# A hybrid attention block on one core: the first MLP in two blocks of two tiles, beside single tiles of projection and memory attention

## The chip, the core and the metric

The kernel runs on one NeuronCore of a Trainium2 chip. Five engines work side by side, each on a queue of its own: TensorE (PE; its weight loads are listed apart as PEld), VectorE (DVE), ScalarE (ACT), GpSimd (POOL) and SyncE (SP), which here only issues DMAs. The metric is the device time of one execution in microseconds. Before the change three runs gave 1806.28 to 1810.84 us, with a median of 1808.53.

## What is computed

One transformer block on x of 1024 tokens by 1024 features, in float32:

```
for l in range(DEPTH):
    x = x + _hybrid_mixer(_rms_norm(x, norm1_g[l]), w_in[l], ..., w_out[l])
    x = x + _memory_xattn(_rms_norm(x, norm2_g[l]), mem, mem_norm_g[l], w_xq[l], w_xk[l], w_xv[l], ..., w_xo[l])
    x = x + _sq_relu_mlp(_rms_norm(x, norm3_g[l]), w_ff_in[l], w_ff_out[l])
```

The mixer has eight heads of indexed sparse attention (for each query the 256 keys with the best index score) and eight heads of block sparse attention in three branches (compressed, selected, window). Its output goes through `w_out` (1024 by 1024). Memory attention has four heads of 128 over 256 memory rows. The MLP is

```
def _sq_relu_mlp(h, w_ff_in, w_ff_out):
    return jnp.square(jax.nn.relu(h @ w_ff_in)) @ w_ff_out
```

with matrices of 1024 by 4096 and 4096 by 1024.

## The kernel before

**Tiles and precision.** Tokens go in eight tiles of 128 rows. A product that needs more than one pass of `fp32r` splits both operands into a high part and a rest: three matmuls, high by high, high by rest, rest by high. `split_w` makes the two parts of a weight: a copy on one engine, and a subtraction on another. The pairs come in turn from a plan; in `PLAN_MAIN` it is ScalarE for the copy ("a") and GpSimd for the subtraction ("g"). `load_w` does this after a DMA of 256 KB into `wraw`. Products for which a weight is not split (`load_whole`) use plain float32 matmuls on the loaded weights; those of `between` and `memory` are such.

**Stages.** `project` of tiles 0 to 3 runs alone. Then `attend` makes attention tile by tile, with the index scores and the top-256 search of the next tile beside it (`index_mask`). The generator `fill` supplies work to stand beside attention: `project` of tiles 4 to 7, `memory` (keys and values of the memory rows, kept in DRAM as `KX` and `VX`), `between` for tiles 0 and 1, `between` for 2 and 3, `mlp` for tiles 0 to 3, `between` for 4 and 5. What `fill` has left when attention ends runs in the tail, together with `between` for tiles 6 and 7, and then `mlp` for tiles 4 to 7.

**`between`** (line 894) takes a stretch of tiles from the attention output in DRAM (`oT_dr`) to the input of the MLP: the product with `w_out` and the residual (`add_to`, line 891), the norm and its transposes (`norm_T2`), the query product with `w_xq`, memory attention for pairs of heads (`memory_item`), a round trip of its output through DRAM (`xo_dr`), and the product with `w_xo`.

**`mlp`** (line 994) runs eight groups of 512 hidden features. For each it computes the hidden features of all its tiles, 24 matmuls of 128x512 for 128 features (three parts by eight slices of 128 input features), then ReLU and square on ScalarE (lines 1026, 1027) and the split on GpSimd (1029, 1030). Then come the two halves of the output, 12 matmuls of 128x512 for each tile, added to the residual.

**Order.** Every stage is a generator that yields an amount of work after each step. `together` steps through attention and lets `fill` go on while its amount is at most attention's times the pace. A tuple from `fill`, `(need, pace)`, holds it until attention is past tile `need`, and sets the new pace. `beside` and `merge` step through two generators in proportion to given totals; in the tail `REST` = 70 stands against 45. The instructions are recorded in that order and then arranged by the framework's scheduler; on the chip each engine runs its own queue in order.

**Memory.** `RINGS` gives the number of buffers for each name in a pool. `dn` holds `fill`'s stages from `memory` on, `d2` the tail's. Accumulators in PSUM are rings too: `dn` uses `psD` (two) and `psM` (one), attention `psS`, `psPT` and `psPV`; in the tail `d2` uses `psS` and `psPT`.

Of the kernel before, what the change touches and what calls it, by code (L numbers as in the profile page):

```python
# [10 lines left out]
F32R = mybir.dt.float32r  # L11
# [32 lines left out]
PLAN_HEAD = ("ag", "av")  # L44
PLAN_MAIN = ("ag",)
PLAN_TAIL = ("ag", "av", "ag")
# [32 lines left out]
TC_ARGS = {"schedule_with_timeline_sim": True}  # L79
PACES = (1.35, 1.35, 1.35, 1.75, 1.75)  # L80
REST = 70.0

# [26 lines left out]

def together(att, fill, projected):  # L110

# [4 lines left out]
    while la:  # L116
        held = part > len(projected)
        if lead is None and need < tile_:
            lead = df - da * pace
        if lf and need < tile_ and (held or df <= lead + da * pace):  # L120
            w = next(fill, None)
            lf = w is not None
            if isinstance(w, tuple):
                need, pace = w
                lead = None
            else:
                df += w or 0.0
        else:
            assert not held
            x = next(att, None)  # L130
            la = x is not None
            if la and x[1] is None:
                part += 1
            elif la:
                tile_ = x[0]
                da += x[1]
# [30 lines left out]
def build(nc, tc, I, C, out):  # L167
# [159 lines left out]

    def xT(pool, nt, whole=False):

        parts = [pool.tile([P, DM // P, nt * P], F32 if whole else F32R, tag="x" + n, name="x" + n)  # L330
                 for n in ("h" if whole else "hl")]
        return (parts, [lambda t, k, x=x: x[:, k, t * P:(t + 1) * P] for x in parts],
# [661 lines left out]
    def mlp(pool, t0, nt, x2s):  # L994
# [13 lines left out]
        for f4 in range(8):  # L1008
# [24 lines left out]
            for c in range(2):  # L1033
# [4 lines left out]
                for t in range(nt):  # L1038
# [12 lines left out]
                    yield 2.6  # L1051

    def pe_stack():
        pe = p1.tile([P, 2, 32], F32, tag="pe", name="pe")
# [33 lines left out]
    aw = aw_pool.__enter__()  # L1088
    projected = []

    def fill():
# [17 lines left out]
    together(attend(aw, st), rest, projected)  # L1109
    aw_pool.__exit__(None, None, None)  # L1110
# [32 lines left out]
```

## Time and profile before

| | |
|---|---|
| median of 3 runs | 1808.53 us |
| profiled execution | 1807.76 us, its span 1806.0 us |
| granted TensorE clock, mean | 0.976 |
| attention's first value product of tiles 0 to 7 | 162, 215, 304, 415, 542, 718, 929, 1155 us |
| last value product of attention | 1304 us |
| DMA traffic | 185.38 MB, mean 103 GB/s |

Times in the profile are microseconds of one execution, unless marked ns; L with a number is a line of the kernel before. Engine rows give busy time, its share of the span and the count of instructions. The slices divide the span into 40; a digit is the busy share in tenths. Rows of windows give, for each stretch, its length, the busy time of each engine with the count of instructions in brackets, then the clock that the throttle granted to TensorE as a share of full speed, the busy share of the DMA engines, and GB/s. Rows of groups name the line, engine and operation, output<-inputs, shapes and count, then the busy time, the mean of one in ns, and the idle time just before them with what ended it. Timeline rows give start, duration, instruction and count; in square brackets is the idle time before it. DMA rows give the KB of each and the median time from issue to landing. Matmuls are pipelined: their distance is read from the starts, not from the mean duration.

### The profile page before, as it was taken

The numbers are of one execution on the slowest core, as the hardware profiler recorded it, in microseconds if no ns is written. First come the engines' busy times: TensorE is split into PE (matmuls) and PEld (weight loads), VectorE is DVE, ScalarE is ACT, GpSimd is POOL, SyncE is SP. The second block draws the span as 40 slices with busy tenths as digits, with TensorE's granted clock in tenths as the row PEclk, the third lists the DMA queues.
The fourth block names the chain that finished last, engine by engine and source line by source line (L and its number), as shares of the span: only waits on it lengthen the run. The fifth ranks groups of instructions, "written<-read, shape, count | busy, mean of one in ns | idle before, by whom it ended". The sixth has DMA issues, their size and how long they took to land. (4 is left out here: it accounts for less than half of the span.)

```text
span 1806.0 us, 27690 instructions
## 1 busy us (share of the span) xinstructions
PE 1700.2 (94%) x9134; PEld 1447.8 (80%) x9134; DVE 927.8 (51%) x2343; ACT 1061.9 (59%) x2655; POOL 887.4 (49%) x1015
## 2 busy tenths in 40 slices
PE   5987999899989999999998999999999799999998
PEld 5986888688878777788886888888888687787887
DVE  4545757665874776375754555646524322222221
ACT  4445669797688579855896558994513333333332
POOL 2356647363541355568575667662111144545444
PEclk9998999999999999999999999999999799999999
DMA  6235221366336211212122212226384122222222
GB/s 193 73 121 155 70 68 58 114 196 175 102 109 196 87 59 42 75 65 80 59 75 75 62 65 78 65 74 194 98 284 151 47 87 89 97 91 96 94 95 93
DMA packets 171887, 185.38 MB, mean 103 GB/s; under 512 B 26464, under 2 KB 140896, under 8 KB 171744
## 3 DMA queue, kind: packets, MB, share of 16 engines
q1 hardware_dynamic: 163808, 173.13, 30.3%
q0 software_dynamic: 7936, 10.49, 2.2%
q8 instruction: 72, 1.18, 0.3%
q14 instruction: 71, 0.58, 0.1%
HBM read 162.59 MB, written 20.97 MB: 102 GB/s over the span
## 5 line engine op out<-in xcount | busy, mean ns | idle before, releaser
L249 POOL TENSOR_TENSOR wlo<-wraw,whi 128x512 fp32r<-128x512 f32 (+1 forms) x231 | 310.6, 1351 | 280.9 <-ACT whi L244 252.9
L244 ACT ACTIVATE whi<-wraw 128x512 fp32r<-128x512 f32 (+2 forms) x289 | 181.0, 628 | 250.8 <-PE psS L218 156.8
L218 PE MATMUL psD<-whi,xh 128*128 128x256 f32 (+1 forms) x704 | 191.1, 352 | 4.4 <-ACT whi L244 3.4
L218 PE MATMUL psD<-wlo,xh 128*128 128x256 f32 (+1 forms) x704 | 190.3, 352 | 1.6 <-DMA wlo<-in_w_in_dram 1.0
L236 DVE TENSOR_TENSOR pl<-psPT,ph 128x512 fp32r<-128x512 f32 (+1 forms) x232 | 142.1, 621 | 78.9 <-ACT ph L235 76.3
L218 PE MATMUL psD<-whi,h 128*128 128x512 f32 x512 | 174.3, 403 | 3.7 <-ACT whi L244 1.6
L218 PE MATMUL psS<-whi,h 128*128 128x512 f32 x512 | 162.4, 392 | 5.4 <-DVE b L891 5.4
L680 ACT ACTIVATE S<-S,mn 128x128 f32<-128x128 f32 (+7 forms) x192 | 142.7, 744 | 40.5 <-DVE mn L678 39.0
L685 POOL TENSOR_SCALAR S<-S,sums,gi 128x640 f32<-128x640 f32 (+7 forms) x128 | 107.8, 853 | 114.1 <-DVE sums L683 103.5
L235 ACT ACTIVATE ph<-psPT 128x512 fp32r<-128x512 f32 (+1 forms) x232 | 122.9, 540 | 61.5 <-PE psPT L695 57.1
L249 DVE TENSOR_TENSOR wlo<-wraw,whi 128x512 fp32r<-128x512 f32 (+1 forms) x58 | 56.3, 971 | 170.3 <-ACT whi L244 170.1
L218 PEld LDWEIGHTS psD<-wlo,xh 128*128 128x128 f32 x704 | 132.4, 193 | 13.6 <-DMA wlo<-in_w_in_dram 1.4
L218 PEld LDWEIGHTS psD<-whi,xh 128*128 128x128 f32 x704 | 130.0, 193 | 14.2 <-ACT whi L244 3.8
L695 PE MATMUL psPT<-c_ident,S 128*128 128x128 f32 x816 | 131.8, 277 | 3.9 <-POOL S L685 2.6
L891 DVE TENSOR_TENSOR b<-psS,b 128x512 f32<-128x512 f32 (+1 forms) x80 | 49.9, 636 | 138.5 <-PE psS L218 138.5
L218 PE MATMUL psS<-K,qh 128*128 128x384 f32 (+3 forms) x288 | 112.4, 394 | 8.9 <-DVE mn L678 3.9
L218 PEld LDWEIGHTS psS<-whi,h 128*128 128x128 f32 x512 | 96.0, 188 | 30.4 <-DVE b L891 10.1
L218 PEld LDWEIGHTS psD<-whi,h 128*128 128x128 f32 x512 | 95.5, 189 | 25.8 <-ACT whi L244 2.0
L695 PEld LDWEIGHTS psPT<-c_ident,S 128*128 128x128 f32 x816 | 97.6, 142 | 14.1 <-POOL S L685 4.5
L218 PE MATMUL psD<-wlo,h 128*128 128x512 f32 x256 | 102.6, 404 | 1.1 <-POOL wlo L249 1.1
L218 PE MATMUL psD<-xh,wlo 128*128 128x512 f32 x256 | 101.5, 398 | 0.0
L891 DVE TENSOR_TENSOR b<-psD,b 128x512 f32<-128x512 f32 (+1 forms) x112 | 63.2, 573 | 74.0 <-PE psD L218 66.9
(289 smaller groups left out, 4546.2 us busy)
## 6 DMA issues: line engine op xcount, KB each, us to landing
wraw<-in_w_ff_in_dram SPq DMA_DIRECT2D x128, 256.0 KB, 2.7
wraw<-in_w_ff_out_dram SPq DMA_DIRECT2D x128, 256.0 KB, 2.6
whi<-in_w_out_dram SPq DMA_DIRECT2D x32, 256.0 KB, 3.8
wlo<-in_w_out_dram SPq DMA_DIRECT2D x32, 256.0 KB, 4.3
wraw<-in_w_in_dram SPq DMA_DIRECT2D x24, 256.0 KB, 3.4
q<-st SPq DMA_DIRECT2D x12, 512.0 KB, 2.6
qin<-q SPq DMA_DIRECT2D x44, 128.0 KB, 2.3
x<-in_x_dram SPq DMA_DIRECT2D x8, 512.0 KB, 5.5
```

Source lines behind the costliest of these rows:

```text
L218: te.matmul(o, a, b, start=start, stop=stop)
L235: s.activation(hi, src, AF.Copy)
L236: v.tensor_tensor(lo, src, hi, op=ALU.subtract)
L244: s.activation(hi, raw, AF.Copy)
L249: (v if l == "v" else g).tensor_tensor(lo, raw, hi, op=ALU.subtract)
L680: s.activation(S, S, AF.Exp, bias=low, scale=-1.0, accum_out=sums[:, hh:hh + 1])
L685: g.tensor_scalar(Ss[hh], Ss[hh], sums[:, hh:hh + 1], 1.0 if gate is None else gate[:, hh:hh + 1], op0=ALU.mult, op1=ALU.mult)
L695: te.transpose(p2[:, j, hh, :], S[:, (c + j) * P:(c + j + 1) * P], ident)
L891: v.tensor_tensor(dst, pt, dst, op=ALU.add)
```

## The change

The first MLP, for tiles 0 to 3 in one pass, becomes two passes of a new function `mlp2`, each for two tiles. `fill` calls `between` for tiles 0 and 1, keeps their residuals in SBUF, and then runs `two_streams`: the main stream is `mlp2` for tiles 0 and 1 and then for 2 and 3; the side stream is `between` for one tile at a time, 2, 3, 4 and 5. The second `mlp2` starts when tiles 2 and 3 are through, and tiles 4 and 5 wait for that start. A side tile starts when attention is past it (`seen["tile"]`). Steps of the two streams are recorded in proportion to their amounts (`SIDE` = 0.9). What is not done when attention ends goes to the tail, against `between` for tiles 6 and 7 and the first 4.0 units of the last MLP.

Beside that: the paces of the last stages go from 1.75 to 1.5, `REST` from 70 to 110; whole weights in `dn` get a ring of their own of two buffers (`wb`) in place of `whi` and `wlo` with four each; `mlp2` has its own rings for the hidden features (`hs`, `mr`); in `PLAN_MAIN` every third subtraction goes to VectorE; and `between` loads attention's output straight into the tile that later holds the norm's transposes.

```diff
-    "dn": {"b4": 4, "h": 8, "relu": 2, "wraw": 2, "whi": 4, "wlo": 4},
+    "dn": {"b4": 4, "h": 7, "hs": 8, "mr": 2, "relu": 2, "wb": 2, "wraw": 2, "whi": 4, "wlo": 4},
-PLAN_MAIN = ("ag",)
+PLAN_MAIN = ("ag", "av", "ag")
-PACES = (1.35, 1.35, 1.35, 1.75, 1.75)
-REST = 70.0
+PACES = (1.35, 1.35, 1.35, 1.5, 1.5)
+SIDE = 0.9
+REST = 110.0
...
-        raw = ring(pool, ("whi", "wlo")[wholes["i"] % 2], shape)
+        raw = ring(pool, "wb" if "wb" in RINGS.get(pool.name, ()) else ("whi", "wlo")[wholes["i"] % 2], shape)
...
     def between(pool, t0, nt, x2s, keep):
-        o_of = []
+        one = "b" if nt == 1 else "h"
+        (o,), xf, _ = xT(pool, nt, True, one)
         for t in range(nt):
-            o = ring(pool, "b4", [P, 8, P])
             for c in range(8):
-                nc.sync.dma_start(o[:, c, :], oT_dr[t0 + t][c])
-            o_of.append(o)
+                nc.sync.dma_start(o[:, c, t * P:(t + 1) * P], oT_dr[t0 + t][c])
...
-        yield from gemm(pool, [lambda t, k: o_of[t][:, k, :]], 8, nt, W["w_out"], four, add_to)
-        _, xf, xt_of = xT(pool, nt, True)
+        yield from gemm(pool, xf, 8, nt, W["w_out"], four, add_to)
+        _, xf, xt_of = xT(pool, nt, True, one)
...
+    def mlp2(pool, t0, x2s):
+        x2 = [x2s[t0], x2s[t0 + 1]]
+        (xh, xl), _, xt_of = xT(pool, 2)
+        gb3 = gain2(pool, W["norm3_g"])
+        for t in range(2):
+            norm_T2(pool, x2[t], gb3, xt_of(t))
+            yield 1.0
+        for f4 in range(8):
+            hs = []
+            for f2 in range(2):
+                gr = []
+                c0 = (f4 * 4 + f2 * 2) * P
+                for k0 in range(0, 8, KG):
+                    hi, lo = load_w(pool, [P, KG, 256], (lambda r: r, W["w_ff_in"][k0 * P:(k0 + KG) * P, c0:c0 + 256]
+                                                         .rearrange("(k p) n -> p k n", p=P)))
+                    gr += [(hi[:, k, :], lo[:, k, :]) for k in range(KG)]
+                for f in range(2):
+                    pt = pst(TAGS[pool.name][0], [P, 256])
+                    fs = slice(f * P, (f + 1) * P)
+                    for k in range(8):
+                        wh, wl = gr[k]
+                        mm(pt, wh[:, fs], xh[:, k, :], k == 0, False)
+                        mm(pt, wl[:, fs], xh[:, k, :], False, False)
+                        mm(pt, wh[:, fs], xl[:, k, :], False, k == 7)
+                    hh, hl = ring(pool, "hs", [P, 256], F32R), ring(pool, "hs", [P, 256], F32R)
+                    r = ring(pool, "mr", [P, 256])
+                    s.activation(r, pt, AF.Relu)
+                    s.activation(r, r, AF.Square)
+                    g.tensor_scalar(hh, r, 1.0, 1.0, op0=ALU.mult, op1=ALU.mult)
+                    g.tensor_tensor(hl, r, hh, op=ALU.subtract)
+                    hs.append((hh, hl))
+                    yield 2.6
+            for c in range(2):
...
+                    gr.append(load_w(pool, [P, 512], (lambda r: r, W["w_ff_out"][r0:r0 + P, cs])))
+                for t in range(2):
+                    pt = pst(TAGS[pool.name][0], [P, 512])
...
+                    v.tensor_tensor(x2[t][:, cs], pt, x2[t][:, cs], op=ALU.add)
...
+                    yield 2.6
...
-        yield from between(dn, 0, 2, {}, False)
-        yield 3, PACES[2]
         x2s = {}
-        yield from between(dn, 2, 2, x2s, True)
-        yield 3, PACES[3]
-        yield from mlp(dn, 0, 4, x2s)
-        yield 5, PACES[4]
-        yield from between(dn, 4, 2, {}, False)
+        yield from between(dn, 0, 2, x2s, True)
+        yield seen["tile"] - 1, PACES[2]
+        yield from two_streams(dn, x2s)
+
+    def two_streams(dn, x2s):
+        main, mains = mlp2(dn, 0, x2s), 1
+        side, t = None, 2
+        dm = ds = 0.0
+        while main or side or mains < 2 or t < 6:
+            if side is None and t < 6 and seen["tile"] > t and (t < 4 or mains == 2):
+                side, ds = between(dn, t, 1, x2s, t < 4), dm
+                if t == 4:
+                    yield seen["tile"] - 1, PACES[3]
+            if main is None and mains == 1 and side is None and t >= 4:
+                main, mains = mlp2(dn, 2, x2s), 2
+            if side and (main is None or ds <= dm):
+                w = next(side, None)
+                ds += (w or 0.0) / SIDE
+                if w is None:
+                    side, t = None, t + 1
+            elif main:
+                w = next(main, None)
+                dm += w or 0.0
+                if w is None:
+                    main = None
+            elif t < 6:
+                w = t, PACES[3]
+            if w is not None:
+                yield w
...
-    merge((rest, REST), (between(d2, 6, 2, x2s, True), 45.0))
+    last = mlp(d2, 4, 4, x2s)
+    merge((rest, REST), (chain(between(d2, 6, 2, x2s, True), take(last, 4.0)), 62.0))
     dn_pool.__exit__(None, None, None)
-    drain(mlp(d2, 4, 4, x2s))
+    drain(last)
```

More of the change, by code (lines that the diff above doesn't have):

```diff
@@ L107, in merge, with together @@
     drain(beside(*a, *b))
-def together(att, fill, projected):
+def together(att, fill, projected, seen):
     da = df = lead = 0.0
@@ L134, in together @@
             elif la:
-                tile_ = x[0]
+                tile_ = seen["tile"] = x[0]
                 da += x[1]
@@ L326, in gemm, with xT @@
                 yield nk * (5 - len(xs)) * w / 2400.0
-    def xT(pool, nt, whole=False):
+    def xT(pool, nt, whole=False, one="h"):
         parts = [pool.tile([P, DM // P, nt * P], F32 if whole else F32R, tag="x" + n, name="x" + n)
-                 for n in ("h" if whole else "hl")]
+                 for n in (one if whole else "hl")]
         return (parts, [lambda t, k, x=x: x[:, k, t * P:(t + 1) * P] for x in parts],
@@ L1051, in mlp @@
                     yield 2.6
+    def mlp2(pool, t0, x2s):
[31 more added lines that the diff above has]
+            for c in range(2):
+                cs = slice(c * 512, (c + 1) * 512)
+                gr = []
+                for k in range(4):
+                    r0 = (f4 * 4 + k) * P
+                    gr.append(load_w(pool, [P, 512], (lambda r: r, W["w_ff_out"][r0:r0 + P, cs])))
+                for t in range(2):
+                    pt = pst(TAGS[pool.name][0], [P, 512])
+                    us = slice(t * P, (t + 1) * P)
+                    for f in range(4):
+                        hh, hl = hs[f]
+                        wh, wl = gr[f]
+                        mm(pt, hh[:, us], wh, f == 0, False)
+                        mm(pt, hh[:, us], wl, False, False)
+                        mm(pt, hl[:, us], wh, False, f == 3)
+                    v.tensor_tensor(x2[t][:, cs], pt, x2[t][:, cs], op=ALU.add)
+                    if f4 == 7:
+                        nc.sync.dma_start(out[0, (t0 + t) * P:(t0 + t + 1) * P, cs], x2[t][:, cs])
+                    yield 2.6
@@ L1089, in build @@
     projected = []
+    seen = {"tile": -1}
     def fill():
@@ L1098, in fill @@
         yield 1, PACES[1]
-        yield from between(dn, 0, 2, {}, False)
-        yield 3, PACES[2]
         x2s = {}
-        yield from between(dn, 2, 2, x2s, True)
-        yield 3, PACES[3]
-        yield from mlp(dn, 0, 4, x2s)
-        yield 5, PACES[4]
-        yield from between(dn, 4, 2, {}, False)
+        yield from between(dn, 0, 2, x2s, True)
[26 more added lines that the diff above has]
+                yield w
     rest = fill()
-    together(attend(aw, st), rest, projected)
+    together(attend(aw, st), rest, projected, seen)
+    seen["tile"] = NT
     aw_pool.__exit__(None, None, None)
```

## The prediction

> **What bounds the kernel now.** I read the page first (busy time, slices, the chain), then TensorE's share stage by stage, then the holes in it.
>
> ```profile
> PE 1700.2 (94%) x9134; PEld 1447.8 (80%) x9134; DVE 927.8 (51%) x2343; ACT 1061.9 (59%) x2655; POOL 887.4 (49%) x1015
> ...
> PE   5987999899989999999998999999999799999998
> ...
> PE 20%; DVE 1%; issue 0%
> ```
>
> TensorE is busy in almost every slice, and the chain that ended last is the tail's second MLP, matmuls alone. So the time is TensorE's work plus the stretches in which it stands still or runs at a lowered clock. A busy PE is not one at its peak, so the granted clock has to be read beside the busy time. I cut the span at the first `psPV<-cph,Vc` of tiles 3 to 7 (the compressed branch's value product), at the end of attention (1304), and where the second MLP's matmuls begin (1440):
>
> ```profile
> core 0: us, PE busy (x) PEld busy (x) DVE busy (x) ACT busy (x) POOL busy (x), PEclk, DMA share, GB/s
> 304.00:415.00 111.00, 98.65 (x521) 83.45 (x520) 77.23 (x214) 95.69 (x300) 62.02 (x90) 0.94 0.44 136
> 415.00:542.00 127.00, 118.59 (x701) 103.15 (x699) 88.03 (x246) 95.77 (x269) 57.00 (x86) 0.99 0.43 130
> 542.00:718.00 176.00, 166.19 (x943) 141.56 (x941) 115.42 (x332) 136.51 (x350) 71.88 (x91) 0.98 0.31 97
> 718.00:929.00 211.00, 206.98 (x1074) 173.24 (x1074) 122.56 (x270) 153.99 (x350) 144.16 (x144) 1.00 0.22 71
> 929.00:1155.00 226.00, 220.60 (x1132) 183.78 (x1131) 125.62 (x289) 160.74 (x356) 146.57 (x146) 0.98 0.21 67
> 1155.00:1304.00 149.00, 146.75 (x834) 127.66 (x832) 88.51 (x217) 95.81 (x206) 61.75 (x65) 0.99 0.37 117
> 1304.00:1440.00 136.00, 121.14 (x600) 103.88 (x598) 50.10 (x129) 37.20 (x86) 19.00 (x28) 0.88 0.53 165
> 1440.00:1806.00 366.00, 356.75 (x1538) 287.68 (x1536) 83.09 (x106) 113.64 (x187) 173.08 (x146) 1.00 0.28 92
> ```
>
> Loss in a row is idle time plus (1 - clock) x length. While the first MLP stands beside attention (718 to 1155) it is 4.0 + 0 and 5.4 + 4.5 us in 437. While projection and memory attention are the only filler it is more: 12.4 + 6.7 in the first row, 9.8 + 3.5 in the third. The largest is the passage from attention to the tail, 1304 to 1440: 14.9 + 0.12 x 136 = 31.2 us. Three holes, and what ends them:
>
> ```profile
> 664.00:700.00 36.00, 31.13 (x175) 25.15 (x176) 32.13 (x91) 34.66 (x89) 15.82 (x23) 0.91 0.07 19
> 1306.00:1324.00 18.00, 15.95 (x64) 13.80 (x65) 2.55 (x7) 2.29 (x6) 3.85 (x8) 0.72 0.94 284
> 1394.00:1442.00 48.00, 36.42 (x157) 29.20 (x158) 21.38 (x47) 16.78 (x35) 6.43 (x8) 0.75 0.20 61
> ...
> 1409.43 1.09 PE L274 MATMUL psPT<-c_ident,relu 128*128 128x128 f32 x4 [3.60 <-DMA relu<-xo]
> ...
> 1411.81 1.92 PE L218 MATMUL psS<-whi,xh 128*128 128x256 f32 x4
> ...
> 1414.56 1.03 PE L218 MATMUL psS<-whi,xh 128*128 128x256 f32 x4
> 1415.42 1.03 PE L218 MATMUL psS<-wlo,xh 128*128 128x256 f32 x4
> ...
> 1429.79 1.30 PE L274 MATMUL psPT<-c_ident,relu 128*128 128x128 f32 x8 [2.98 <-DVE relu L297]
> ```
>
> From 1394 tiles 6 and 7 go alone through a serial chain (memory attention's round trip through `xo`, the last norm); TensorE waits 3.60 and 2.98 us, and after the first of these four matmuls take 1.92 us in place of 1.03. From 1306 to 1324 the DMA engines are 0.94 busy: that hole is the tail's first loads. From 664 to 700 no filler is left and ScalarE is busy 34.66 of 36.
>
> **The change part by part.** *Tail, gain.* In the built program's order 480 half-width and 288 full-width matmuls of the first MLP now stand behind attention's last product, mixed with what is left of tile 5 and with tiles 6 and 7; before there were none. Their price needs the spacing of issues:
>
> ```profile
> 60.00:68.00 8.00, 8.00 (x73) 8.00 (x72) 6.80 (x24) 4.67 (x18) 4.22 (x4) 1.00 0.25 76
> ...
> 1559.68 44.12 PE psS L218 x191
> ```
>
> A 512-wide matmul costs 44.12/191 = 0.231 us; at 256 wide, in the projection's dense stretch, 8.00/73 = 0.110, its 72 weight loads included. The moved MLP work is about 480 x 0.115 + 288 x 0.231 = 122 us, four times the 31.2 us of loss. The first hole stays, since tiles 6 and 7 still start their loads when attention's buffers are freed: 2.0 + 0.28 x 18 = 7.1 us. That leaves 24; the serial steps are in order on TensorE's queue and still stop it at times, so I take 18 (bounds 0 and 24).
>
> *Hold at tile 4, gain.* The MLP's first matmul now stands 145 matmuls behind tile 4's first compressed value product, before 799. The hole of 664 to 700 is 4.9 + 0.09 x 36 = 8.1 us; I take 8. Nothing is the lower bound (ScalarE is full there with or without MLP), all 13.3 us of tile 4's row the upper one.
>
> *Half-width matmuls.* The input half of the first MLP goes from 768 matmuls of 512 to 1536 of 256: at half of 0.231 nothing, at 0.110 it gains 8 us. If every weight load had to be waited for it would be 1536 x 0.193 - 768 x 0.231 = +119 (193 ns is the mean of a load in the rows below), but the dense row has 72 loads in 8 us with TensorE never idle. I take 0, bounds -8 and +8.
>
> *Splitting weights twice.* Each of the two blocks loads and splits all of both matrices:
>
> ```profile
> L249 POOL TENSOR_TENSOR wlo<-wraw,whi 128x512 fp32r<-128x512 f32 (+1 forms) x231 | 310.6, 1351 | 280.9 <-ACT whi L244 252.9 <-DMA wraw<-in_w_ff_in_dram 23.9 <-PE psS L218 2.2
> L244 ACT ACTIVATE whi<-wraw 128x512 fp32r<-128x512 f32 (+2 forms) x289 | 181.0, 628 | 250.8 <-PE psS L218 156.8 <-DMA wraw<-in_w_ff_in_dram 49.1 <-PE psD L218 13.2
> L249 DVE TENSOR_TENSOR wlo<-wraw,whi 128x512 fp32r<-128x512 f32 (+1 forms) x58 | 56.3, 971 | 170.3 <-ACT whi L244 170.1
> L218 PEld LDWEIGHTS psD<-wlo,xh 128*128 128x128 f32 x704 | 132.4, 193 | 13.6 <-DMA wlo<-in_w_in_dram 1.4 <-ACT relu L413 1.2
> L218 PE MATMUL psD<-wlo,h 128*128 128x512 f32 x256 | 102.6, 404 | 1.1 <-POOL wlo L249 1.1
> L1027 ACT ACTIVATE relu<-relu 128x512 f32<-128x512 f32 x64 | 40.0, 626 | 0.7
> L401 ACT ACTIVATE st<-psD 128x256 f32<-128x256 f32 x48 | 17.9, 380 | 21.5 <-PE psD L218 18.6 <-DMA q<-st 2.6
> L921 POOL DMA_DIRECT2D h<-KX x16 | 9.2, 575 | 22.3 <-PE psS L218 11.5 <-PE psD L218 10.8
> ...
> 304.00:1304.00 1000.00, 957.75 (x5197) 812.85 (x5195) 617.37 (x1565) 738.52 (x1825) 543.38 (x619) 0.98 0.31 96
> ```
>
> ScalarE: 128 more copies x 0.628 = 80 us; squares and relus, 128 of 256 wide for 64 of 512, 128 x 0.380 - 64 x 0.626 = +9. The subtractions go from 128 on GpSimd to 171 there and 85 on VectorE: +43 x 1.351 = 58 and 85 x 0.971 = 83. One-tile passes add 16 loads of K and V on GpSimd's queue, 9 us, and behind a waiting one stand the subtractions. Two thirds of the first MLP stay in attention (1056 half and 480 full of 1536 and 768), so ScalarE has there 2/3 x (120 + 89) = 139 us of MLP for 120 before (128 x 0.628 + 64 x 0.626), in a stretch that gets some 100 us shorter (122 us of MLP leave it): from 738.5/1000 to about 758/900 = 0.84. That is near the first row's 0.86, where 17% was lost, and far above the 0.71 and 0.73 at which 437 us lost 14. But 664 to 700 aside the first row's loss also has the change of fillers in it. I take 5 us; bounds 0 and 30 (6% more of tiles 4 to 6).
>
> A row and a rule beside this. Where a subtraction on GpSimd met a two-operand VectorE instruction it took 2.31 us, not 1.35:
>
> ```profile
> 976.99 2.31 POOL L249 TENSOR_TENSOR wlo<-wraw,whi 128x512 fp32r<-128x512 f32 x1 [1.32 <-ACT whi L244]
> ...
> 976.18 2.02 DVE L652 TENSOR_TENSOR_SCAN isc<-tkh 128x896 f32<-128x896 bf16 x1
> ```
>
> The Trainium skill's "SBUF — State Buffer", section "SBUF: two separate sides", says that a VectorE operation with two SBUF inputs and a GpSimd operation take one port pair as an exclusive lock, and the later one blocks wholly. The pair of rows agrees. By the rule each of the 85 subtractions moved to VectorE would be such an operation and this term would be larger; that is the third rival.
>
> *Two buffers for whole weights.* Projection and memory attention in `dn` loaded their weights into eight buffers (`whi`, `wlo`); now into two (`wb`), 176 loads in all, 64 more than before because single tiles load everything again.
>
> ```profile
> whi<-in_w_out_dram SPq DMA_DIRECT2D x32, 256.0 KB, 3.8
> wlo<-in_w_out_dram SPq DMA_DIRECT2D x32, 256.0 KB, 4.3
> ...
> wraw<-in_w_ff_out_dram SPq DMA_DIRECT2D x128, 256.0 KB, 2.6
> ```
>
> A full-precision matmul runs as two passes of (1415.42 - 1414.56)/4 = 0.215 us, so a load feeds a single tile for 4 x 0.215 = 0.86 us, and it can only be issued when the last but one has been read. In the built order I summed the matmuls between a buffer's last reader and its next load's first reader, at the spacings above and 15% stretched: the median is 3.4 to 3.9 us up to tile 4, the least 0.9. Where that is under the landing time TensorE stands, with attention queued behind the waiting matmul; carrying each stall forward, the sum is 13 us if a load lands in 2.6 and 45 in 3.8. Part falls where TensorE waits anyway. I take 11, nearer to 2.6 because the queue is shallow; bounds 0 and 45.
>
> *Sum.* 1807.8 (the profiled execution; its span 1806.0 and 1.8 around it) - 18 - 8 + 0 + 5 + 11 = **1798 us**. The median of the runs is 1808.5, 0.7 above that execution.
>
> **Rivals.** *The side stream stops the main one (slower).* Side and main share two `psD` accumulators in turn, and a side accumulator is held through its four `wb` loads. If a load takes 3.8 us or more, MLP groups wait for the side's accumulator as well. Then the ring costs its 45, crowding 15, the tail's gain stays at 18 and tile 4's goes: 1807.8 - 18 + 60 = 1850 at worst, **1828** with half of the excess hidden. For it: 2.6 to 4.3 us landings against 0.86 us of work. Against: before tile 4 TensorE lost 19 us in 111 anyway, so there is room. It decides from about 21 us of stall.
>
> *The work only moves.* TensorE's matmul work is the same. If the tail's serial steps block the MLP queued behind them, the gain is eaten by the second split: **1808**. For it: 96% busy in 304 to 1304 already. Against: 1394 to 1442 has 11.6 us idle and nothing queued.
>
> *The lock.* 85 subtractions, each holding GpSimd 2.31 - 1.35 = 0.96 us longer, are 82 us of GpSimd, busy 144 of 211 in tile 5; if a fifth of it reaches TensorE, 1798 + 16 = **1814**. Against: in its 256 matmuls on `wlo` in the output half TensorE waited 1.1 us for it.
>
> That the change does not do what it says is excluded by the built order above.
>
> **How the numbers follow.** Forecast 0.45, side stream 0.28, only moved 0.19, lock 0.08. A change below 0.3% (5.4 us) can't be told from none here. The forecast's own range is 1780 to 1806, from its bounds: faster in 0.42 and same in 0.03 of all; only-moved gives 0.06 faster, 0.09 same, 0.04 slower; side stream and lock are slower but for 0.02 same. Together faster 0.48, same 0.14, slower 0.38. For 8 in 10 the range reaches to 1772 (tail 24, tile 4 13, nothing lost) and, into the side stream's case, to 1835.
>
> **What would show it.** Right: behind attention's end the granted clock is over 0.95 except in the first 20 us; attention ends near 1210; no clock drop in tile 4. Wrong: TensorE's waits headed by `DMA wb`, or by a `psD` group waiting for the side; ScalarE over 0.9 with TensorE's idle time over 5% in tiles 4 to 6; half-width groups of 24 taking over 2.9 us.

## The result, and the profile after

| | kernel before | changed kernel |
|---|---|---|
| median of 4 runs | 1808.43 us | 1936.53 us |
| lowest to highest | 1806.28 to 1810.84 | 1928.09 to 1938.99 |
| span of the profiled execution | 1806.0 us | 1937.1 us |
| granted TensorE clock, mean | 0.976 | 0.972 |
| attention's last value product ends | 1304 us | 1337 us |
| DMA traffic | 185.38 MB | 239.55 MB |

The ratio is 1.07 (95% interval 1.0662 to 1.0737): 128 us slower, where 10 us faster was forecast. The page of the changed kernel: busy time by engine, the slices of TensorE and its clock, and the chain that ended last.

```profile
PE 1750.5 (90%) x9902; PEld 1499.5 (77%) x9902; DVE 995.9 (51%) x2429; ACT 1139.0 (59%) x2847; POOL 967.1 (50%) x1137
...
PE   5979999888878999799978899998999999999999
...
PEclk9988999999999999899999999999999999999999
...
PE 19%; DMA 1%; POOL 1%; DVE 0%; issue 0%; ACT 0%; ACTq 0%; POOLq 0%
```

TensorE is busy 90% of the span where it had 94%, and ScalarE, the busiest of the others, still has 59%. The loss is in the slices: from the eighth digit to the 28th (a slice is 48.4 us) TensorE has many eights and sevens where it had nines. The chain still ends in the second MLP and tells nothing of it. The same stages as in the prediction, cut at the starts of the tiles in the changed kernel, with the whole stretch beside attention ahead of them:

```profile
core 0: us, PE busy (x) PEld busy (x) DVE busy (x) ACT busy (x) POOL busy (x), PEclk, DMA share, GB/s
306.00:1337.00 1031.00, 907.05 (x5322) 775.18 (x5322) 648.53 (x1624) 759.33 (x1911) 531.97 (x651) 0.97 0.40 125
...
550.00:753.00 203.00, 174.94 (x1030) 150.74 (x1030) 122.33 (x317) 147.43 (x377) 88.89 (x116) 0.97 0.44 134
753.00:946.00 193.00, 173.05 (x1034) 149.97 (x1032) 125.32 (x298) 136.42 (x329) 107.96 (x126) 0.95 0.39 122
946.00:1186.00 240.00, 210.94 (x1234) 177.48 (x1235) 149.24 (x333) 176.39 (x409) 146.69 (x161) 0.97 0.38 119
1186.00:1337.00 151.00, 138.24 (x887) 122.87 (x885) 95.24 (x229) 111.81 (x252) 67.34 (x76) 0.99 0.45 142
1337.00:1545.00 208.00, 192.45 (x1071) 165.54 (x1072) 69.90 (x140) 77.70 (x161) 87.68 (x93) 0.97 0.56 178
1545.00:1937.00 392.00, 383.11 (x1703) 312.00 (x1701) 100.53 (x120) 129.46 (x218) 196.47 (x172) 1.00 0.31 102
```

The tail is longer by 600 - 502 = 98 us, and holds the 480 half-width and 288 full-width matmuls that were to be moved, 122 us at the prediction's prices. But work went the other way too. These are the matmuls of `between` for tiles 4 and 5 (on `psD`) that stand behind attention, first in the kernel before (1304 to 1806), then in the changed one (1337 to 1938):

```profile
L218 PE MATMUL psD<-whi,xh 128*128 128x256 f32 x48 | 13.7, 411 | 0.0
...
L218 PE MATMUL psD<-wlo,xh 128*128 128x256 f32 x48 | 13.2, 400 | 0.0
L218 PE MATMUL psD<-h 128*128 128x128 f32 (+1 forms) x64 | 12.1, 342 | 1.8 <-ACT h L235 1.5 <-DVE h L236 0.2
```

```profile
L219 PE MATMUL psD<-wb,xb 128*128 128x256 f32 x32 | 8.0, 383 | 1.0 <-DMA wb<-in_w_xo_dram 1.0
...
L219 PE MATMUL psD<-h 128*128 128x128 f32 (+1 forms) x18 | 3.1, 301 | 1.2 <-ACT h L236 1.2
```

Some 64 full-precision passes at 0.215 us and 46 matmuls on `psD<-h` at about 0.11, near 20 us by this estimate, left the tail. So about 102 us of work came to it on balance, and the move won 4 us; the loss in the rows (21.8 us in 1337 to 1545, for 31.2 before) falls by 9. The fault lies ahead of the tail. At these prices attention was to end near 1202 (the prediction said 1210); it ends at 1337, some 135 us later. In 306 to 1337 TensorE is idle for 1031 - 907 = 124 us and loses 0.03 x 1031 = 31 to the clock, 155 in all. Before, 304 to 1304 lost 42 + 20 = 62. That is 93 of the 135 us; the other 40 stand in TensorE's busy time, and no run takes them apart. What TensorE waited for from tile 4 to attention's end (us in total, times, longest), first in the kernel before, for 542 to 1304, then in the changed one, for 550 to 1337:

```profile
PE psS L218 <- DVE mn L678: 2.8, 5, 1.0
PE psS L218 <- ACT ir L604: 2.1, 2, 1.4
PE psPV L218 <- DVE pl L236: 1.8, 4, 0.7
PE psD L218 <- ACT whi L244: 1.6, 1, 1.6
...
PE psD L218 <- POOL wlo L249: 1.1, 2, 0.6
```

```profile
PE psD L219 <- DMA wb<-in_w_out_dram: 10.2, 10, 2.4
PE psD L219 <- POOL wlo L250: 10.2, 15, 2.2
PE psS L219 <- DVE mn L679: 8.4, 13, 1.1
PE psM L275 <- DMA relu<-xo: 8.0, 4, 4.5
PE psD L219 <- ACT whi L245: 7.4, 12, 1.3
PE psPV L219 <- DVE pl L237: 5.0, 8, 1.3
PE psD L219 <- DMA wb<-in_w_xq_dram: 4.8, 6, 1.3
PE psD L219 <- ACT mr L1081: 4.3, 7, 0.8
```

The whole weights (`wb`, with a third row of 2.2 us for `w_xo`) and the MLP's split weights (`wlo` and `whi`) weigh about the same, 17.2 and 17.6 us. One step further back, what ScalarE waited for beside attention before it could copy a weight. The first fence is the kernel before (304 to 1304), the second the changed one (306 to 1337).

```profile
ACT whi L244 <- DMA wraw<-in_w_ff_in_dram: 14.4, 14, 2.9
...
ACT whi L244 <- DMA wraw<-in_w_ff_out_dram: 10.5, 13, 2.0
```

```profile
ACT whi L245 <- DMA wraw<-in_w_ff_in_dram: 45.7, 30, 5.7
...
ACT whi L245 <- DMA wraw<-in_w_ff_out_dram: 31.2, 31, 3.6
```

ScalarE is not crowded: it stands still for 77 us, before for 25, because a raw weight has not landed. (Over the whole run it is 218 for 60, but 141 and 35 of these lie in the tail, where TensorE waited only 3.6 us for split weights in the changed kernel.) The DMA engines don't hold the weights up: a load lands in 2.8 to 2.9 us in the median, before in 2.6 to 2.7. That gives a theory which the prediction did not have. A raw buffer (`wraw`, two of them) is held while a weight lands (2.7 us, the median of before), while ScalarE copies it (0.63) and while GpSimd subtracts (1.35), 4.7 us. Two buffers so give a weight every 2.35 us at best. In the MLP of four tiles a weight feeds 12 matmuls of 512, 12 x 0.231 = 2.8 us; in a block of two tiles half of that, 1.4 us. So the supply was enough for the block of four tiles, and would not be enough for one of two. So far this is argued, not shown.

### The profile page after: what moved, and what is told of

It reads as the page before. It is cut to its first block, busy times and chain, and to the rows that moved or that the text cites. A ratio compares the mean times of both kernels' runs of the same rounds, so it can differ in the third digit from the quotient of the medians.

```text
span 1937.1 us, 30190 instructions
## 1 busy us (share of the span) xinstructions
PE 1750.5 (90%) x9902; PEld 1499.5 (77%) x9902; DVE 995.9 (51%) x2429; ACT 1139.0 (59%) x2847; POOL 967.1 (50%) x1137
## 2 busy tenths in 40 slices
DMA packets 218524, 239.55 MB, mean 124 GB/s; under 512 B 29824, under 2 KB 177024, under 8 KB 218368
## 5 line engine op out<-in xcount | busy, mean ns | idle before, releaser
L250 POOL TENSOR_TENSOR wlo<-wraw,whi 128x512 fp32r<-128x512 f32 (+2 forms) x273 | 363.2, 1337 | 374.7 <-ACT whi L245 355.5
L245 ACT ACTIVATE whi<-wraw 128x512 fp32r<-128x512 f32 x417 | 259.5, 627 | 373.3 <-PE psS L219 129.2
L250 DVE TENSOR_TENSOR wlo<-wraw,whi 128x512 fp32r<-128x512 f32 x144 | 136.2, 946 | 285.3 <-ACT whi L245 280.2
L219 PE MATMUL psD<-whi,hs 128*128 128x512 f32 x512 | 184.0, 420 | 8.3 <-ACT whi L245 3.3
L219 PE MATMUL psD<-xh,whi 128*128 128x256 f32 x512 | 148.9, 299 | 8.3 <-ACT whi L245 4.6
L219 PE MATMUL psD<-xh,wlo 128*128 128x256 f32 x512 | 149.0, 295 | 7.2 <-POOL wlo L250 5.6
L219 PE MATMUL psD<-wb,xb 128*128 128x256 f32 x512 | 135.8, 395 | 20.3 <-DMA wb<-in_w_out_dram 10.2
L219 PE MATMUL psD<-xl,whi 128*128 128x256 f32 x512 | 144.6, 286 | 0.0
L219 PEld LDWEIGHTS psD<-whi,hs 128*128 128x128 f32 x512 | 100.0, 198 | 32.6 <-ACT whi L245 5.4
L219 PE MATMUL psD<-wb,xh 128*128 128x256 f32 x384 | 100.5, 410 | 20.9 <-DMA xh<-o 5.6
```

Source lines behind the costliest of these rows:

```text
L219: te.matmul(o, a, b, start=start, stop=stop)
L245: s.activation(hi, raw, AF.Copy)
L250: (v if l == "v" else g).tensor_tensor(lo, raw, hi, op=ALU.subtract)
```

## Experiments: one part after another

Two theories stood at the outset. *Supply*: the halved MLP can't be fed. *Sharing*: the prediction's first rival, the side stream stops the main one through `wb` and the shared `psD`. In the texts put down before each run *supply* is theory B, and *sharing* theory A (or C, where the shared accumulators alone are meant). An edit can also change the order in which the framework's scheduler puts the instructions (in e5 below 1824 of the first MLP's 2304 matmuls come before attention's end, in e7 all of them), so a difference of some 10 us between two runs may be one of order.

**Changed kernel, streams taken apart, and three single parts of it.**

```diff
 e1_seq
-        yield seen["tile"] - 1, PACES[2]
-        yield from two_streams(dn, x2s)
+        yield 3, PACES[2]
+        yield from between(dn, 2, 2, x2s, True)
+        yield 3, PACES[3]
+        yield from mlp2(dn, 0, x2s)
+        yield from mlp2(dn, 2, x2s)
+        yield 5, PACES[4]
+        yield from between(dn, 4, 2, {}, False)
 e2_nowb
-    "dn": {"b4": 4, "h": 7, "hs": 8, "mr": 2, "relu": 2, "wb": 2, "wraw": 2, "whi": 4, "wlo": 4},
+    "dn": {"b4": 4, "h": 7, "hs": 8, "mr": 2, "relu": 2, "wraw": 2, "whi": 5, "wlo": 5},
 e3_side_m: around next(side)
+                TAGS["dn"] = ("M", "M")
                 w = next(side, None)
+                TAGS["dn"] = ("D", "M")
 e4_plan_ag
-PLAN_MAIN = ("ag", "av", "ag")
+PLAN_MAIN = ("ag",)
```

> The changed kernel with its two streams taken apart: the MLP of tiles 0 to 3 stays in two blocks of two tiles, but the passes from attention to the MLP go in pairs of tiles and one after the other, as before the change. Theory A (the side stream's own waits stop TensorE's queue all through attention): without it the loss goes back, 1800 to 1835 us. Theory B (halved blocks can't be supplied: each weight is split for half as many matmul columns, so TensorE waits for ScalarE, GpSimd and VectorE): 1880 to 1940, and waits on wlo and whi of 15 us or more while the MLP stands beside attention. Theory C (main and side share two accumulators): as A.

> The changed kernel, but whole weights go through the rings whi and wlo again (five buffers each) and the ring wb of two is gone. Theory A in the form of the prediction's first rival (two buffers are the cause): 1850 to 1890, waits on whole weights under 8 us in place of some 27. Theory A in the form that single tiles in series are the cause whatever their buffers: 1915 to 1950. Theories B and C: 1915 to 1950.

> The changed kernel, but the side stream takes its accumulators from psM, so that the MLP has both psD accumulators for itself. Theory C (shared accumulators): 1840 to 1890. Theories A and B: 1925 to 1960, since the side stream then has one accumulator for all and gets slower.

> The changed kernel with all weight subtractions in attention on GpSimd again. The lock of the prediction's third rival: 1900 to 1925, faster than the changed kernel, as VectorE's two-operand subtractions leave GpSimd's port. Theory B: 1945 to 1990, since GpSimd then has 128 subtractions more than before the change alone. Theory A: 1930 to 1950, little changed.

| run | median | before, same chip | ratio (95%) | against the changed kernel |
|---|---|---|---|---|
| e1_seq | 1987.67 | 1812.71 | 1.0976 (1.0923 to 1.1029) | +51 |
| e2_nowb | 1921.64 | 1812.71 | 1.0612 (1.0557 to 1.0667) | -15 |
| e3_side_m | 1909.63 | 1812.71 | 1.0545 (1.0465 to 1.0626) | -27 |
| e4_plan_ag | 1949.09 | 1812.71 | 1.0763 (1.071 to 1.0817) | +13 |

The last column compares medians of two chips; the kernel before is 4 us slower on the chip of these runs. With the streams one after the other there is nothing for the side to stop, and the kernel is slower still, above every range that was expected: sharing is not the main cause, and standing side by side wins some 51 us, though the changed kernel pays for single tiles as well and e1 goes by pairs. Buffers and accumulators do cost, 15 and 27 us, the second between the ranges of the theories. Giving all subtractions back to GpSimd loses 13. The 15 and the 13 are near the noise: the intervals of e2 and e4 touch that of the changed kernel (1.0662 to 1.0737).

**The kernel before, with the halved MLP or the single tiles alone.**

```diff
 e5_half
-        yield from mlp(dn, 0, 4, x2s)
+        yield from mlp(dn, 0, 2, x2s)
+        yield from mlp(dn, 2, 2, x2s)
 e6_single
-        yield from between(dn, 2, 2, x2s, True)
+        yield from between(dn, 2, 1, x2s, True)
+        yield from between(dn, 3, 1, x2s, True)
...
-        yield from between(dn, 4, 2, {}, False)
+        yield from between(dn, 4, 1, {}, False)
+        yield from between(dn, 5, 1, {}, False)
```

> The kernel before with one part of the change alone: the MLP of tiles 0 to 3 runs as two calls for two tiles each, all rings, paces and stages as before. Theory B, now with a place (two raw buffers: a weight's load lands 2.7 us after its issue and is held until copied and subtracted, 2 us more, so two buffers give a weight every 2.4 to 2.8 us; one of four tiles feeds 24 x 0.231 / 2 = 2.8 us of matmuls, one of two tiles 1.4): 1900 to 2000 us, with the first MLP drawn out to some 256 x 2.6 = 670 us or more. Theory A (side stream and single tiles): 1800 to 1830.

> The kernel before with the other part alone: tiles 2, 3, 4 and 5 pass projection and memory attention one by one, one after the other, with the rings of before. Theory B: 1805 to 1835 (64 more loads, each pass with the latency of a single tile). Theory A with single tiles as the cause: 1850 to 1900.

The halved MLP alone: 1935.58 us against 1813.98, ratio 1.0672 (1.0641 to 1.0703), +122. The single tiles alone: 1866.24, ratio 1.029 (1.026 to 1.032), +52, where *supply* expected at most 1835: they are a cause of their own. The first of the two has almost the whole of the result. Its MLP, windows of the kernel before (first MLP matmul to the last) and of e5:

```profile
694.00:1229.00 535.00, 525.58 (x2729) 439.83 (x2728) 302.96 (x686) 398.49 (x901) 350.13 (x350) 0.99 0.22 70
```

```profile
676.00:1447.00 771.00, 688.75 (x4171) 590.21 (x4170) 389.88 (x880) 534.43 (x1231) 564.86 (x584) 0.97 0.39 118
```

535 us become 771, the last 169 of them behind attention's end at 1278, and idle time goes from 9 to 82 us. Other matmuls run in both windows, attention's above all, so a weight was needed less often than its own matmuls say: 128 weights in 535 us are one every 4.2 us, and two buffers could give that. Twice as many in the same time would be one every 2.1 us, which is under the 2.35 that they give at best; it came to 771/256 = 3.0. What ScalarE and TensorE waited for in e5, from 676 to 1447:

```profile
ACT whi L244 <- DMA wraw<-in_w_ff_in_dram: 88.6, 59, 7.2
ACT whi L244 <- DMA wraw<-in_w_ff_out_dram: 78.8, 65, 4.3
```

```profile
PE psD L218 <- POOL wlo L249: 37.5, 51, 3.0
PE psD L218 <- ACT whi L244: 14.7, 23, 2.1
```

In the MLP of the kernel before (694 to 1229) the same rows are 14.4 and 10.5 us for ScalarE, 1.1 and 1.6 for TensorE.

In the run with single tiles the loss has another place. Its window of tile 4:

```profile
545.00:733.00 188.00, 160.53 (x842) 134.08 (x839) 111.16 (x321) 125.11 (x323) 65.52 (x90) 0.90 0.47 143
```

27.5 idle and 0.10 x 188 at the clock are 46 us, where tile 4 lost 13. Its weights had all eight buffers here. TensorE's longest wait in this stretch is for the round trip through `xo` (5.1 us, before 0.6), then come attention's own splits (3.4 and 2.7, before 1.1 and 0.3) and the norm with its transposes (2.5 and 2.2, before 0.9 and 1.4); the granted clock is 0.90, before 0.98. This fits a serial chain that a pair of tiles goes through once and two single tiles go through twice; no run takes it apart further.

**More raw buffers, more split buffers, less GpSimd.** All three on the halved MLP of e5.

```diff
-    "dn": {"b4": 4, "h": 8, "relu": 2, "wraw": 2, "whi": 4, "wlo": 4},
+    "dn": {"b4": 4, "h": 8, "relu": 2, "wraw": 4, "whi": 4, "wlo": 4},     (e7)
+    "dn": {"b4": 4, "h": 8, "relu": 2, "wraw": 4, "whi": 7, "wlo": 7},     (e8)
-PLAN_MAIN = ("ag",)
+PLAN_MAIN = ("ag", "av", "ag")     (e10, on e7)
+PLAN_MAIN = ("ag", "av")           (e14, on e7)
```

> e5 with four raw buffers in place of two, nothing else. Theory B by raw buffers: most of e5's loss goes, 1810 to 1860 us. Were it the split itself (ScalarE, GpSimd) or the rings of split weights: within 15 us of e5.

> e7 with seven buffers each for the split weights in place of four. Theory B by raw buffers alone: within 10 us of e7. If the four split buffers hold the splits back too (a group of 24 matmuls reads all four, so that the next four can only be made while the second half of it runs): 20 us or more below e7.

> e7 (halved blocks alone, four raw buffers) with every third subtraction of attention's stretch on VectorE, as in the change. If GpSimd is the next limit of the supply (its busy share was 0.85 in tiles 5 and 6 of e7): 1840 to 1865 us, and GpSimd under 0.75 there. If VectorE's two-operand subtractions lock it out: 1880 or more.

> The kernel before with the MLP in two blocks, four raw buffers, and every second subtraction on VectorE (every third one gave +35 us, none +68). Supply theory: what is left over the width's 14 us is still GpSimd's part, so +20 to +30. If VectorE's own load and the port they share have become the limit, no gain or a loss: +33 to +45.

| run | median | ratio (95%) | over before |
|---|---|---|---|
| e5: 2 raw buffers | 1935.58 | 1.0672 (1.0641 to 1.0703) | +122 |
| e7: 4 raw buffers | 1881.85 | 1.0376 (1.0345 to 1.0407) | +68 |
| e8: and 7 + 7 split buffers | 1886.45 | 1.0401 (1.0337 to 1.0465) | +72 |
| e10: e7, every third subtraction on VectorE | 1846.31 | 1.0201 (1.0136 to 1.0267) | +35 |
| e14: e7, every second | 1852.29 | 1.0227 (1.0208 to 1.0247) | +40 |

Supply is shown from both ends. Two more raw buffers win 54 us (*supply* had expected more, 1810 to 1860). In the MLP of e7, 680 to 1321, ScalarE's waits for raw weights fall from 167.4 to 3.7 us, and TensorE's for split weights from 52.2 to 1.9, nearly as much as the time:

```profile
ACT whi L244 <- DMA wraw<-in_w_ff_out_dram: 2.1, 3, 1.5
ACT whi L244 <- DMA wraw<-in_w_ff_in_dram: 1.6, 2, 1.0
```

```profile
PE psD L218 <- POOL wlo L249: 1.9, 3, 1.1
```

Then the next in the row sets the pace. GpSimd (the fifth column of engines) is busy 187 of 218 us in tile 5 of e7, 0.86 of the time:

```profile
711.00:929.00 218.00, 197.05 (x1252) 174.71 (x1251) 125.39 (x267) 168.83 (x400) 187.29 (x197) 0.97 0.38 114
```

Moving a third of its subtractions wins some 33 us (GpSimd is then busy 171 of 223 us in that tile, 0.77); moving half wins no more, so GpSimd is no longer the limit at +35 to +40. The +40 lie in the range expected for VectorE as the next limit; this is not shown further: in e14 TensorE's waits behind 718 are spread over VectorE (`pl` 6.6 us, `b` 3.9) and GpSimd (3.4 and 3.3). More split buffers change nothing that can be measured.

**The width of the matmuls alone.** The kernel before, with its weights loaded once, the input half in two passes of 256 columns.

```diff
-                    for k in range(8):
+                    for a0 in range(0, nt * P, 256 if pool.name == "dn" else nt * P):
+                        cc = slice(a0, a0 + (256 if pool.name == "dn" else nt * P))
+                        for k in range(8):
...
-                        mm(pt, wh[:, fs], xh[:, k, :], k == 0, False)
+                            mm(pt[:, cc], wh[:, fs], xh[:, k, cc], k == 0, False)
```

> The kernel before, in which the input half of the first MLP is computed in two passes of 256 columns over weights that are loaded and split once: 1536 matmuls of 256 in place of 768 of 512, no further load, no further split. Theory B (the supply of split weights is what halving costs): 1808 to 1822 us. If the half-width matmuls or their weight loads cost by themselves: 1850 or more.

1825.40 us against 1811.24, ratio 1.0086 (1.0052 to 1.0119): +14 us for 768 more matmuls and weight loads. The matmuls themselves are the smaller part of it. TensorE's busy time rises by 5 us (1700.2 to 1705.2 in the profiled executions) and its idle time by 12, and a single wait in the tail, for a load of `w_out`, is 8.6 us (0.5 before):

```profile
PE psD L218 <- DMA whi<-in_w_out_dram: 8.6, 1, 8.6
```

If the 14 us hold in the halved MLP too, then of its +122, after 54, 33 and 14, about 20 are left without a cause.

**The changed kernel, fed better.**

```diff
 e11_changed_raw3
-    "dn": {"b4": 4, "h": 7, "hs": 8, "mr": 2, "relu": 2, "wb": 2, "wraw": 2, "whi": 4, "wlo": 4},
+    "dn": {"b4": 4, "h": 6, "hs": 8, "mr": 2, "relu": 2, "wb": 2, "wraw": 3, "whi": 4, "wlo": 4},
 e12_changed_raw4_m, with the two TAGS lines of e3
+    "dn": {"b4": 4, "h": 7, "hs": 8, "mr": 2, "relu": 2, "wraw": 4, "whi": 4, "wlo": 4},
```

> The changed kernel with three raw buffers in place of two (paid for with one buffer of h, six in place of seven). Theory B by raw buffers: 1895 to 1925, and fewer waits of ScalarE's copies for raw weights. If the raw buffers matter only where MLP stands alone: 1925 to 1945.

> The changed kernel with the side stream's accumulators in psM (as e3), whole weights in whi and wlo in place of wb, and four raw buffers. If raw buffers and shared accumulators are causes that add up: 1850 to 1890. If e3's gain already was that of the supply: 1900 to 1915.

Three raw buffers in the changed kernel: 1904.97 us, ratio 1.0525 (1.0479 to 1.0572), 32 us better than the change. Four, without the `wb` ring and with the side's accumulators in `psM`: 1849.42, ratio 1.0218 (1.0144 to 1.0293), 87 us better. Beside attention ScalarE's waits for raw weights fall from 77 us to 23 in the first and to 3 in the second. The second has three edits at once, of which e2 and e3 had measured 15 and 27. So the cause found in e5 to e7 works in the changed kernel as well. The second is still 38 us over before.

**What no run had alone yet.** The direct load of attention's output, the tail's order and the paces; and whether GpSimd limits the kernel before too.

```diff
 e17_direct_load (in e15 and e16 too)
-            o = ring(pool, "b4", [P, 8, P])
+        (o,), xf, _ = xT(pool, nt, True)
...
-        yield from gemm(pool, [lambda t, k: o_of[t][:, k, :]], 8, nt, W["w_out"], four, add_to)
+        yield from gemm(pool, xf, 8, nt, W["w_out"], four, add_to)
 e18_tail_only (in e15 and e16 too)
-REST = 70.0
+REST = 110.0
-    merge((rest, REST), (between(d2, 6, 2, x2s, True), 45.0))
+    last = mlp(d2, 4, 4, x2s)
+    merge((rest, REST), (chain(between(d2, 6, 2, x2s, True), take(last, 4.0)), 62.0))
...
-    drain(mlp(d2, 4, 4, x2s))
+    drain(last)
 e15_rest_of_change, e16_rest_av: both, and
-PACES = (1.35, 1.35, 1.35, 1.75, 1.75)
+PACES = (1.35, 1.35, 1.35, 1.5, 1.5)
 e13_before_av, and in e16
-PLAN_MAIN = ("ag",)
+PLAN_MAIN = ("ag", "av", "ag")
```

> The kernel before with one edit: every third subtraction of the first MLP's split goes to VectorE. If the four-tile MLP is balanced (2.8 us of matmuls for each load, and a buffer gives a weight in about that time), GpSimd doesn't limit it and the time stays within 5 us of before. If GpSimd limited there too, 10 to 30 us are gained.

> The kernel before with the parts of the change that no run had alone: paces 1.5, the tail's proportion 110, the first four steps of the last MLP beside tiles 6 and 7, and the load of attention's output into the tile of the transposes. Supply theory: none of it touches a weight, so 1803 to 1811 (the four norms in the tail can give a few us, against the 2.98 us wait). If the order in the tail is a cost of its own, over 1815.

> The rest of the change and every third subtraction on VectorE, without blocks and without single tiles. The sum of the two runs before: 1800 to 1810. It would be the faster kernel if either of them is under before.

> The kernel before with one edit: attention's output is loaded straight into the tile that later holds the norm's transposes. The rest of the change together gave +25 us. If the shared tile is the cause (a stretch's loads wait until the stretch or MLP before has read its tile, and TensorE waits for them), this alone gives +10 to +25. If the paces are, under +5.

> The kernel before with the tail's part alone: proportion 110 for 70, and the first four steps of the last MLP (its norms) beside tiles 6 and 7. No MLP matmuls are moved. It could fill the 2.98 us wait for the last norm and the lowered clock behind it: 1803 to 1809. If the tail's order is what costs in the rest of the change, 1815 to 1835.

| run | median | before, same chip | ratio (95%) |
|---|---|---|---|
| e13_before_av | 1827.02 | 1812.68 | 1.0086 (1.007 to 1.0101) |
| e15_rest_of_change | 1837.53 | 1812.68 | 1.0151 (1.0131 to 1.0172) |
| e16_rest_av | 1833.13 | 1812.68 | 1.0117 (1.0099 to 1.0134) |
| e17_direct_load | 1837.32 | 1811.42 | 1.0138 (1.0119 to 1.0157) |
| e18_tail_only | 1815.46 | 1811.42 | 1.002 (1.0008 to 1.0033) |

The rest of the change costs 25 us, against the expectation, and the direct load alone has all of that (26 us), an edit to which the prediction gave no term. Its DMAs of attention's output (duration, first and last start), in the kernel before and in e17:

```profile
L900 SPq DMA_DIRECT2D b<-o x64: 319/430/963, 362.3 to 1313.6; - x64
```

```profile
L899 SPq DMA_DIRECT2D xh<-o x64: 319/430/1340, 418.2 to 1334.3; - x64
```

Before, the first stretch's loads go out at 362, into tiles of their own. In e17 they go out at 418, 56 us later: the tile that they fill, `xh`, also serves `memory` ahead of them. The second stretch's go out at 551 for 449, behind the first stretch's use of it. The MLP begins 15 us later (709 for 694), and tile 4 loses 19.2 + 0.04 x 179 = 26 us in place of 13:

```profile
545.00:724.00 179.00, 159.83 (x904) 136.09 (x905) 117.47 (x337) 134.53 (x346) 64.59 (x86) 0.96 0.29 89
```

The waits of TensorE for these loads themselves are short (2.1 us up to tile 4); how the late start becomes 26 us at the end isn't shown step by step. In the changed kernel the edit is not quite the same: only half of these loads go to `xh` (the first at 428 us), those of the single tiles to a tile `xb` of their own (the first at 361), so the 26 us need not hold there.

The tail alone costs 4 us. The paces, what is left, nothing that can be told. Moving subtractions to VectorE costs 14 us where GpSimd is not the limit, and it wins where it is. Why it costs is not shown (GpSimd's own subtraction takes no longer, 1341 ns in e13 for 1351), and together with the rest of the change (e16) the 14 us don't come on top. No version that ran beats the kernel before.

## Why the prediction was wrong, point by point

**Splitting weights twice (+5, bounds 0 and 30): the step that failed.** It asked whether ScalarE and GpSimd would be too busy, by sums of busy time, and they were not (ScalarE 759 of 1031 us, GpSimd 532). It never asked how fast a weight comes through the two raw buffers against how long its matmuls last. Nearly all numbers for that stood in its own rows: 2.6 us to land, 0.63 and 1.35 to split, 0.231 for a matmul, so 2.8 us of matmuls in a block of four tiles and 1.4 in one of two. The halved MLP alone measured +122, of which 54 are raw buffers and some 33 GpSimd.

**Single tiles had no term beyond their weights' buffers** and 9 us of loads on GpSimd's queue. e6, with all eight buffers, measured +52. By its waits the serial chain of projection, norm and memory attention runs twice, with half the matmuls to stand in it.

**The direct load had no term at all:** +26 in the kernel before (e17), not measured alone in the changed one. A buffer saved had been the buffer in which the next loads were waiting.

**Two whole-weight buffers (+11, 0 to 45):** 15 measured in e2, with intervals that touch. Right as far as that shows. The shared `psD`, in the first rival, was worth 27 (e3). That rival had the right side, but its parts come to 42 of 128 us (it feared 60), and without them e12 with four raw buffers is still slower than before.

**Half-width matmuls (0, -8 to +8):** +14 in e9, outside the bounds, but only 5 of it are busy time of TensorE. As the price of the matmuls the term is not refuted; what the run has beyond that is waiting, most of it one load in the tail.

**The hold at tile 4 (-8, 0 to 13.3): failed.** The MLP does begin earlier, at 604 for 694 (185 matmuls behind tile 4's first value product in the trace, where the prediction had 145), but tile 4 lost 28 us idle and 6 at the clock, for 13. The hole was filled with work that was itself waiting.

**Tail (-18, 0 to 24): within the bounds, but too large.** It won 4 us by the work on balance, 9 by the loss in the rows (15.6 + 6.2 in 1337 to 1545, for 31.2). The 768 matmuls moved exactly as the order said; the some 20 us of tiles 4 and 5 that went the other way were not in the sum.

**The lock (1814): fell as to its sign.** Giving the 85 subtractions back to GpSimd lost 13 us (e4, near the noise), and moving them to VectorE won 33 in e10, clear of it. GpSimd's mean subtraction is 1337 ns in the changed kernel, with 144 on VectorE, and 1351 before, with 58. The Trainium skill, "SBUF — State Buffer", section "SBUF: two separate sides", states a lock that makes the later one wait wholly. The single pair of rows in the prediction agreed with it; the mean over 273 shows no such price here. With 187 on VectorE it is 1389 (e14), 38 ns more, against the 960 that the rival took for each of its 85.

```profile
L250 POOL TENSOR_TENSOR wlo<-wraw,whi 128x512 fp32r<-128x512 f32 (+2 forms) x273 | 363.2, 1337 | 374.7 <-ACT whi L245 355.5
```

**The signs that were named.** From tile 4 to attention's end TensorE's waits are headed by `DMA wb`, as a sign of being wrong, with `wlo` level; ScalarE over 0.9 did not come (0.73 in tile 4). Of the 44 half-width groups beside attention 41 took over 2.9 us (median 4.8), but attention's matmuls stand between theirs, and so they do in e9 (50 of 64). The clock behind attention's end is 0.97 and 1.00, as forecast. Attention ends at 1337, not 1210, and that one number places the error ahead of the tail. The upper end of the gains was also added up wrongly: 1807.8 - 24 - 13 is 1771, not 1772.

The parts measured alone (halved MLP 122, single tiles 52, direct load 26, `wb` 15, shared accumulators 27, tail 4, less 13 for the subtractions) come to 233 us; the change measured 128. They may overlap, since several stall the same stretches, the side stream fills some of the holes (51 us in e1), and the direct load may cost less there. How the difference divides among these stays open, and so does the cause of the last 20 us of the halved MLP.

## What to carry to other kernels

When a tile block is made smaller so that weights are read again, compare the time that one weight's matmuls last with the time that one weight needs through its ring of buffers (landing + each step of the split, divided by the buffers); busy shares don't show that limit, since every engine on the way looks half idle. With attention beside it, take the time between two weights in the kernel as it runs (4.2 us), not that of their matmuls alone. Look at what an engine off the critical path waits for, in the stretch that lost time and not in the whole run: ScalarE's wait for raw weights pointed to the cause, while TensorE's own list in the changed kernel had several causes side by side and became plain only when the halved MLP ran alone. A buffer that is merged with another to save room takes the prefetch with it, and needs a term of its own in the sum.

## What the runs showed of the hardware that was not expected

The same edit, every third subtraction from GpSimd to VectorE, was worth -33 us with four raw buffers and a halved MLP (e7 to e10), -13 in the changed kernel (e4, near the noise), and +14 in the kernel before (e13). Halving the width of 768 matmuls at the same total work raised TensorE's busy time by 5 us from one profiled execution to the other (e9), about 6 ns for each of the 768 that came on top; the rest of the +14 us was waiting.
